# One turn per query block, and measured durations in the planner that orders the matmul engine's work

## The chip, the cores and the metric

The kernel runs on one core of a Trainium2 chip. The metric is the device time of one execution in microseconds (us), the median over repeated runs. The engines are named as in the profile: PE (TensorE, matmuls), PEld (its weight loads), DVE (VectorE), ACT (ScalarE), POOL (GpSimd), SP (SyncE, DMA issue).

## The reference

One decoder layer over 1024 positions of width 1024, in float32: a gated DeltaNet mixer (4 heads of 128) and a sparse attention mixer (8 heads of 64 in 2 groups) run side by side on the same normed input, are merged under two gates, and a SwiGLU feed-forward block follows.

```python
h = rms_norm(x, mix_norm_gain)
proj = jnp.einsum('bsd,de->bse', h, w_in)
...
o_a = gated_delta_rule_chunked(q_a, k_a, v_a, beta, log_decay)
...
q_n = partial_rope(q_b.reshape(...), pos) * (NSA_HEAD_DIM ** -0.5)
o_b = native_sparse_attention(q_n, k_cmp, v_cmp, k_slc, v_slc, k_win, v_win, gates, ...)
merged = (jax.nn.sigmoid(merge_a) * jnp.einsum('bse,ed->bsd', o_a, w_branch_gdn)
          + jax.nn.sigmoid(merge_b) * jnp.einsum('bse,ed->bsd', o_b, w_branch_nsa))
x = x + jnp.einsum('bsd,de->bse', merged, w_out)
```

The attention has three branches per block of 128 queries and group: 63 compressed blocks, the selected blocks (with 16 of 16 blocks chosen, that is all keys up to the query) and a window of 512. The scale 64 ** -0.5 is 0.125.

## The kernel before

Products are made at float32 accuracy from a high and a low part: `split` (L83) rounds a value to fp32r on ACT and subtracts it on DVE, and `mmk` (L144) multiplies high by high, high by low and low by high. Three matmuls of one such step, L147 to L149, are called a triple here.

The stages follow one another: norm and first projections; convolution inputs; the DeltaNet chunks; the compressed keys; attention; merge, output projection and feed-forward. Three of them, from some 205 to 925 us, are woven. PE is the one engine whose order the kernel writes itself (`manual_schedule`); the other engines' instructions are placed by a scheduler that takes them in the order in which the program issues them. In a woven stage several Python generators issue work, and `weave` (L205) decides which goes next by `Model` (L180), a small clock of the engines: a generator yields the time at which its next PE work can start, and `weave` takes the one with the earliest start. `m.run(engine, ready, duration)` (L187) books a duration on an engine and returns when the result is there. A filler, the last argument, goes in wherever it can start before all others. The fillers are triples of the projections (`projections`, L703, tile `pn`) and of the merge gates (`gates_half`, L717, tile `pm`), and `mm3g` (L155) tells the model what a triple costs. The durations are numbers in the code, and no time is measured when the kernel is built.

- In the DeltaNet stage `prepare_chunks` (L501) turns and normalises keys and queries of a chunk of 128 positions, `solve_chunks` (L606) makes three rounds of turn (X), product masked on DVE (Pm) and update (Y), `scan_chunks` (L632) carries the state, `turn_chunks` (L687) turns the result. The sums behind Y's start are made on DVE by many small instructions (Ut, Yb). `EV` (L499) is the model's time for an eviction.
- In the compressed stage `compressed` (L789) runs, with the filler; what is left of the projections and of the first half of the gates is issued without cover at its end.
- In attention `all_keys` (L960), `all_queries` (L989), `scores` (L1024), `transposes` (L1117) and `products` (L1146) are woven. A unit is one query block, group and branch. Its scores go to PSUM slots (tag S, six), DVE takes the maximum, ACT the exponential, POOL scales by one over the sum, PE turns the probabilities (`ppt`), `split` makes two parts and PE multiplies both with the values (`po`). At most three turned tiles may be pending. Up to 11 tiles of the second half of the gates (`aside`, L913) are the filler; four more come after attention.
- A query block (128 queries, 4 heads of one group) is loaded as `qraw`, rotated on POOL, scaled there, split into `qs` (twice the same 64 columns side by side, high and low part apart), turned by PE in two groups of four transposes (`pqt`), and copied by ACT into `qt`.

Of the kernel before, what the change touches and what calls it, by code (L numbers as in the profile page):

```python
# [11 lines left out]
F32 = mybir.dt.float32  # L12
# [3 lines left out]
ALU = mybir.AluOpType  # L16
# [17 lines left out]
def tile_hybrid(ctx: ExitStack, tc: tile.TileContext, a: dict, out: bass.AP, dbg=None):  # L34
# [252 lines left out]
    def hN(n):  # L287
        return lambda k: tuple(t[:, k, :] for t in hT2[n])
# [414 lines left out]
    def projections():  # L703
        for c0, n in segs:
            wh, wl = piece()
            for i in range(NT):
                pt = psM("pn")
                yield from mm3g(pt[:, :n], hT(i), lambda k: (wh[:, k, :], wl[:, k, :]), KD, 110)
                st = sp.tile([P, 320], F32, tag="zz", name="nst", bufs=2)
                nc.scalar.copy(st[:, :n], pt[:, :n])  # L710
                o = (i % 2) * P
                nc.gpsimd.dma_start(nsa_d[i // 2][o:o + P, c0 - SEG0:c0 - SEG0 + n], st[:, :n])
        yield from gates_half(0, psM)
# [3 lines left out]
    def gates_half(n, ptile):  # L717
        for pc_ in range(8):
            wh, wl = piece()
            for j in range(2):  # L720
                pt = ptile("pm")
                yield from mm3g(pt, lambda k: (wh[:, k, j * P:(j + 1) * P], wl[:, k, j * P:(j + 1) * P]),
                                hN(n), KD, 216)
                th = stage[0]("thm")
                nc.scalar.activation(th, pt, AF.Tanh, scale=0.5)  # L725
                nc.gpsimd.dma_start(gt_d[2 * pc_ + j][n], th)
                yield 0, 600 if n else 0
# [214 lines left out]
    with ExitStack() as ph:  # L942
# [17 lines left out]
        def all_keys():  # L960
            for i in range(NT):
# [16 lines left out]
                for g in range(2):  # L978
                    yield max(t0, slots["S"][0])
                    t = m.run("pe", max(t0, slots["S"].pop(0)), 120)  # L980
# [4 lines left out]
                    t = m.run("act", t, 270)  # L985
# [3 lines left out]
        def all_queries():  # L989
            for i in range(NT):  # L990
                for g in range(2):
# [9 lines left out]
                    qs = at_("qs", [P, 4, 2, 2, 64], 1, F32R)  # L1001
                    nc.gpsimd.tensor_scalar(raw, raw, 0.125, 1.0, op0=ALU.mult, op1=ALU.mult)
                    qv = qv[:, :, None, :].broadcast_to([P, 4, 2, 64])
                    split(qs[:, :, 0], qs[:, :, 1], qv)
# [6 lines left out]
                    t = m.run("act", m.t["pe"] + 4000, 480)  # L1011
                    t0 = m.run("dve", t, 600)
                    for l in range(2):
                        yield max(t0, slots["S"][0])
                        t = m.run("pe", max(t0, slots["S"].pop(0)), 230)
                        pt = pT("pqt2")
                        for h in range(4):
                            nc.tensor.transpose(pt[:, h, :], qs[:, h, l].bitcast(F32), ident)
                        nc.scalar.copy(qt[:, :, l, :], pt)
                        t = m.run("act", t, 480)  # L1020
                        slots["S"].append(t)
                    qts[2 * i + g] = (qt, ga, t)

        def scores():  # L1024
            for u, (i, g, br, j0, nk) in enumerate(units):
# [10 lines left out]
                if br == 0:  # L1036
# [10 lines left out]
                    t = m.run("dve", t, 340)  # L1047
# [4 lines left out]
                    t = m.run("act", t, 800)  # L1052
                    slots["S"].append(t)
                else:
                    b = 0 if br == 1 else 1
                    cuts = (0, w) if nk <= 4 else (0, (nk + 1) // 2 * P, w)
                    for n in range(len(cuts) - 1):
# [7 lines left out]
                        for h in range(4):  # L1065
# [4 lines left out]
                            t = m.run("pe", t, 2 * (c1 - c0) * 0.42 + 60)  # L1070
# [9 lines left out]
                            t = m.run("dve", t, (c1 - c0) * 1.05 + 70)  # L1080
                            t = m.run("act", t, (c1 - c0) * 0.83 + 140)
# [24 lines left out]
                for n in range(len(cuts) - 1):  # L1106
                    for h in range(4):
                        v = Ps[n][h]
                        nc.gpsimd.tensor_scalar(v, v, cs[:, h, n:n + 1], 1.0, op0=ALU.mult, op1=ALU.mult)  # L1109
                        t = m.run("pool", t, (cuts[n + 1] - cuts[n]) * 1.05 + 30)  # L1110
# [6 lines left out]
        def transposes():  # L1117
            po = None
            for u, (i, g, br, j0, nk) in enumerate(units):
# [4 lines left out]
                for j in range(nk):  # L1124
# [4 lines left out]
                    t = m.run("pe", max(t_p, slots["S"].pop(0)), 230)  # L1129
# [8 lines left out]
                    t = m.run("act", t, 480)  # L1138
                    t = m.run("dve", t, 600)
# [6 lines left out]
        def products():  # L1146
            po = None
            n = 0
            while n < sum(u[4] for u in units):
# [12 lines left out]
                if fin is not None:  # L1162
# [8 lines left out]
                    t = m.run("act", t, 480)  # L1171
                    t = m.run("dve", t, 600)
# [515 lines left out]
```

## Time and profile before

| | |
|---|---|
| median of 3 runs | 1800.11 us (1800.06 to 1801.05) |
| profiled execution | 1798.52 us |
| its span, first to last instruction | 1796.8 us |
| PE busy | 1722.6 us, 96% of the span, 9348 matmuls |
| PEld, DVE, ACT, POOL busy | 1458.3, 1096.6, 768.2, 641.4 us |
| mean granted clock of TensorE | 0.990 of full speed (2.4 GHz) |

A row of the profile names line, engine, operation, output and inputs of a group of instructions. Matmuls are pipelined and their ends are modelled, so printed durations of neighbours overlap: how long a matmul holds PE is read from the start of the next one. In the timeline, brackets give the idle time of the engine just before the row and what ended it. The granted clock is a mean over a stretch.

### The profile page before, as it was taken

What the parts mean: (1) busy time and instruction counts of PE and PEld (TensorE: products, weight loads), DVE (VectorE), ACT (ScalarE), POOL (GpSimd) and SP (SyncE); (2) the same over time, 40 slices, a digit from 0 to 9 for tenths busy, and PEclk for the clock granted to TensorE, in tenths of its full rate; (3) what the DMA queues carried; (4) which work ended last, traced back from release to release, by engine and by line L of the source; (5) the groups of instructions that cost most, each with busy time, mean ns of one, the idle gap of its engine ahead of it and who ended that gap; (6) DMA issues with size and microseconds to landing.
All of it is one profiled execution on the core that took longest, in us unless ns stands there. A gap on an engine that the chain in (4) does not pass through costs nothing.

```text
span 1796.8 us, 26109 instructions
## 1 busy us (share of the span) xinstructions
PE 1722.6 (96%) x9348; PEld 1458.3 (81%) x9348; DVE 1096.6 (61%) x2061; ACT 768.2 (43%) x1814; POOL 641.4 (36%) x1028
## 2 busy tenths in 40 slices
PE   7999989999999899999999999899999999989998
PEld 7888878989888677777778888688888888878886
DVE  6466566664543688677744434665555555678685
ACT  5244433343321698777732212433333333344452
POOL 3400144344231886675530211644444344210000
PEclk9999999999999999999999999899999999999999
DMA  6322444443473312011057350033333333572342
GB/s 208 99 96 95 143 118 110 109 121 78 110 194 105 107 34 60 25 42 39 13 178 227 109 201 1 13 120 113 95 104 119 95 106 100 186 276 85 100 140 100
DMA packets 183009, 196.40 MB, mean 109 GB/s; under 512 B 23408, under 2 KB 139360, under 8 KB 182880
## 3 DMA queue, kind: packets, MB, share of 16 engines
q1 hardware_dynamic: 164112, 162.03, 29.7%
q0 software_dynamic: 18560, 32.62, 6.1%
q8 instruction: 73, 1.20, 0.3%
q14 instruction: 56, 0.46, 0.1%
q10 hardware_dynamic: 208, 0.09, 0.0%
HBM read 139.01 MB, written 55.69 MB: 108 GB/s over the span
## 4 chain that ended last, share of the span: by engine, by line
PE 75%; issue 6%; DVE 6%; POOL 5%; ACT 3%; DMA 3%; SPq 0%; POOLq 0%; DVEq 0%; ACTq 0%
PE M L149 14%; PE M L147 14%; PE M L148 14%; PE s L1074 3%; PE ppt L1132 3%; PE pq L148 2%; PE pq L147 2%; PE pq L149 2%; PE po L1159 2%; PE po L1160 2%; PE pm L147 1%; DVE Ut L596 1%; PE pm L149 1%; PE pm L148 1%; PE py L627 1%
## 5 line engine op out<-in xcount | busy, mean ns | idle before, releaser
L85 ACT ACTIVATE ahi<-fraw 128x512 fp32r<-128x512 f32 x88 | 55.6, 633 | 142.0 <-PE M L148 140.1
L1079 ACT ACTIVATE Ps<-s,mx 128x384 f32<-128x384 f32 (+3 forms) x192 | 106.0, 560 | 23.7 <-DVE mx L1078 22.6
L86 DVE TENSOR_TENSOR ptl<-ppt,pth 128x512 fp32r<-128x512 f32 (+1 forms) x148 | 99.0, 683 | 25.0 <-ACT pth L85 24.7
L1109 POOL TENSOR_SCALAR Ps<-Ps,cs 128x384 f32<-128x384 f32 (+3 forms) x192 | 107.9, 580 | 13.3 <-ACT pth L85 5.3
L1078 DVE TENSOR_REDUCE mx<-s 128x1 f32<-128x384 f32 (+3 forms) x192 | 94.9, 514 | 19.0 <-PE s L1077 13.5
L1074 PE MATMUL s<-KT,qt 128*128 128x384 f32 (+3 forms) x384 | 99.3, 359 | 3.0 <-DVE ptl L86 1.8
L147 PE MATMUL pn<-whi,h 128*128 128x264 f32 (+1 forms) x320 | 100.6, 314 | 0.0
L85 ACT ACTIVATE pth<-ppt 128x512 fp32r<-128x512 f32 (+1 forms) x148 | 87.1, 604 | 23.7 <-PE ppt L1132 23.2
L147 PE MATMUL pm<-h,whi 128*128 128x512 f32 x224 | 96.4, 430 | 0.2 <-ACT thm L725 0.2
L148 PE MATMUL pn<-wlo,h 128*128 128x264 f32 (+1 forms) x320 | 91.4, 286 | 0.0
L149 PE MATMUL pn<-whi,h 128*128 128x264 f32 (+1 forms) x320 | 91.3, 285 | 0.0
L149 PE MATMUL pm<-h,wlo 128*128 128x512 f32 x224 | 88.5, 395 | 0.0
L148 PE MATMUL pm<-h,whi 128*128 128x512 f32 x224 | 88.1, 393 | 0.0
L85 ACT ACTIVATE ahi<-fsum 128x512 fp32r<-128x512 f32 x66 | 41.7, 633 | 107.8 <-PE M L148 107.8
L86 DVE TENSOR_TENSOR wlo<-wraw,whi 128x1024 fp32r<-128x1024 f32 (+1 forms) x50 | 61.1, 1232 | 41.2 <-ACT whi L85 39.5
L86 DVE TENSOR_TENSOR alo<-fraw,ahi 128x512 fp32r<-128x512 f32 x88 | 71.3, 811 | 23.5 <-ACT ahi L85 23.4
L1611 POOL TENSOR_TENSOR rms_r<-rms_ms,small 128x1 f32<-128x1 f32 x8 | 5.1, 646 | 209.2 <-DVE rms_ms L1609 209.2
L147 PE MATMUL M<-act,ahi 128*128 128x512 f32 x194 | 77.0, 397 | 2.7 <-ACT ahi L85 2.7
L1132 PE MATMUL ppt<-ident,Ps 128*128 128x128 f32 x528 | 77.7, 274 | 1.5 <-POOL Ps L1109 1.3
L148 PE MATMUL M<-act,ahi 128*128 128x512 f32 x194 | 76.9, 396 | 2.2 <-DVE act L86 2.2
L85 ACT ACTIVATE ahi<-ar 128x512 fp32r<-128x512 f32 x66 | 41.5, 630 | 83.7 <-PE M L148 44.9
L149 PE MATMUL M<-act,alo 128*128 128x512 f32 x194 | 77.0, 397 | 0.0
(509 smaller groups left out, 5515.2 us busy)
## 6 DMA issues: line engine op xcount, KB each, us to landing
wraw<-in_w_in_dram SPq DMA_DIRECT2D x50, 512.0 KB, 4.3
fraw<-in_w_gate_up_dram SPq DMA_DIRECT2D x44, 512.0 KB, 4.1
ar<-act_d SPq DMA_DIRECT2D x35, 512.0 KB, 3.5
act_d<-asum SPq DMA_DIRECT2D x44, 256.0 KB, 2.4
act_d<-act SPq DMA_DIRECT2D x33, 256.0 KB, 2.0
gt_d<-thm POOLq DMA_DIRECT2D x32, 256.0 KB, 2.8
gg<-gt_d SPq DMA_DIRECT2D x32, 256.0 KB, 2.9
qkv_d<-ac POOLq DMA_DIRECT2D x24, 256.0 KB, 2.3
```

The costliest lines, as they stand in the source:

```text
L85: nc.scalar.activation(hi, src, AF.Copy)
L86: nc.vector.tensor_tensor(lo, src, hi.bitcast(F32), op=ALU.subtract)
L147: nc.tensor.matmul(ps, ah, bh, start=first, stop=False)
L148: nc.tensor.matmul(ps, ah, bl, start=False, stop=False)
L149: nc.tensor.matmul(ps, al, bh, start=False, stop=last)
L1074: nc.tensor.matmul(s, qt[:, h, l, :], KT[g][:, b, j0 * P + c0:j0 * P + c1], start=l == 0, stop=l == 1 and not ext)
L1078: nc.vector.tensor_reduce(mx[:, h, n:n + 1], s, axis=AX.X, op=ALU.max, negate=True)
L1079: nc.scalar.activation(pr, s, AF.Exp, bias=mx[:, h, n:n + 1], accum_out=sums[:, h, n:n + 1])
L1109: nc.gpsimd.tensor_scalar(v, v, cs[:, h, n:n + 1], 1.0, op0=ALU.mult, op1=ALU.mult)
L1132: nc.tensor.transpose(pt[:k, h, :], prs[h][:, jj * P:jj * P + k], ident)
L1159: nc.tensor.matmul(po, v, th_, start=first, stop=False)
L1160: nc.tensor.matmul(po, v, tl_, start=False, stop=fin is not None)
```

## The change

Two things. A query block is no longer scaled on POOL and split before it is turned: one ACT copy scales it and writes it twice side by side, PE turns it once in full float32, and `split` makes the two parts as it leaves PSUM. And the numbers of the model change: the cost of a filler triple, and most durations of the attention stage.

```diff
-                yield from mm3g(pt[:, :n], hT(i), lambda k: (wh[:, k, :], wl[:, k, :]), KD, 110)
+                yield from mm3g(pt[:, :n], hT(i), lambda k: (wh[:, k, :], wl[:, k, :]), KD, 121)
...
-                                hN(n), KD, 216)
+                                hN(n), KD, 227)
...
-                    qs = at_("qs", [P, 4, 2, 2, 64], 1, F32R)
-                    nc.gpsimd.tensor_scalar(raw, raw, 0.125, 1.0, op0=ALU.mult, op1=ALU.mult)
-                    qv = qv[:, :, None, :].broadcast_to([P, 4, 2, 64])
-                    split(qs[:, :, 0], qs[:, :, 1], qv)
+                    qs = at_("qs", [P, 4, 2, 64], 1)
+                    nc.scalar.activation(qs, qv[:, :, None, :].broadcast_to([P, 4, 2, 64]), AF.Copy, scale=0.125)
...
-                    t = m.run("act", m.t["pe"] + 4000, 480)
-                    t0 = m.run("dve", t, 600)
-                    for l in range(2):
-                        yield max(t0, slots["S"][0])
-                        t = m.run("pe", max(t0, slots["S"].pop(0)), 230)
-                        pt = pT("pqt2")
-                        for h in range(4):
-                            nc.tensor.transpose(pt[:, h, :], qs[:, h, l].bitcast(F32), ident)
-                        nc.scalar.copy(qt[:, :, l, :], pt)
-                        t = m.run("act", t, 480)
-                        slots["S"].append(t)
+                    t0 = m.run("act", m.t["pe"] + 4000, 600)
+                    yield max(t0, slots["S"][0])
+                    t = m.run("pe", max(t0, slots["S"].pop(0)), 430)
+                    pt = pT("pqt2")
+                    for h in range(4):
+                        nc.tensor.transpose(pt[:, h, :], qs[:, h], ident)
+                    split(qt[:, :, 0, :], qt[:, :, 1, :], pt)
+                    t = m.run("act", t, 610)
+                    t = m.run("dve", t, 685)
+                    slots["S"].append(t)
...
-                            t = m.run("pe", t, 2 * (c1 - c0) * 0.42 + 60)
+                            t = m.run("pe", t, 2 * max(110, (c1 - c0) * 0.43 + 7) + 40 * len(ext))
...
-                            t = m.run("dve", t, (c1 - c0) * 1.05 + 70)
-                            t = m.run("act", t, (c1 - c0) * 0.83 + 140)
+                            t = m.run("dve", t, (c1 - c0) * 1.04 + 150)
+                            t = m.run("act", t, (c1 - c0) * 0.82 + 480)
...
-                        t = m.run("pool", t, (cuts[n + 1] - cuts[n]) * 1.05 + 30)
+                        t = m.run("pool", t, (cuts[n + 1] - cuts[n]) * 0.85 + 280)
...
-                    t = m.run("pe", max(t_p, slots["S"].pop(0)), 230)
+                    t = m.run("pe", max(t_p, slots["S"].pop(0)), 435)
...
-                    t = m.run("act", t, 480)
-                    t = m.run("dve", t, 600)
+                    t = m.run("act", t, 610)
+                    t = m.run("dve", t, 685)
```

The last pair stands in `transposes` and again in `products`; in `all_keys` 120 and 270 become 220 and 380, and in the compressed branch of `scores` 340 and 800 become 420 and 2000.

The numbers move the instructions. Three places are shown, each before and after the change; lines of the changed kernel from L1000 on are three lower.

First piece: DVE in the middle of the DeltaNet stage, where a chunk's keys and queries are normalised (ss, kh, qh) while an earlier chunk is solved (Pm, Y). Before:

```order
L86 TENSOR_TENSOR wlo<-wraw,whi 128x1024
L596 TENSOR_TENSOR Ut<-U,Yb_881 32x13x13
L86 TENSOR_TENSOR wlo<-wraw,whi 128x1024
L598 TENSOR_REDUCE Yb_881<-Ut 32x13
L539 SCALAR_TENSOR_TENSOR ss<-ss,rscale 128x8
L623 TENSOR_TENSOR Pm<-pp,LM 128x512
L596 TENSOR_TENSOR Ut<-U,Yb_881 32x14x14
L86 TENSOR_TENSOR at_4223<-pat,at_4222 128x512
L598 TENSOR_REDUCE Yb_881<-Ut 32x14
L544 TENSOR_TENSOR kh<-pk,rr 128x512
L596 TENSOR_TENSOR Ut<-U,Yb_881 32x225
L628 TENSOR_TENSOR Y<-Y,py 128x512
```

After:

```order
L596 TENSOR_TENSOR Ut<-U,Yb_881 32x14x14
L598 TENSOR_REDUCE Yb_881<-Ut 32x14
L623 TENSOR_TENSOR Pm<-pp,LM 128x512
L596 TENSOR_TENSOR Ut<-U,Yb_881 32x225
L539 SCALAR_TENSOR_TENSOR ss<-ss,rscale 128x8
L598 TENSOR_REDUCE Yb_881<-Ut 32x15
L544 TENSOR_TENSOR kh<-pk,rr 128x512
L86 TENSOR_TENSOR at_4148<-pat,at_4147 128x512
L546 TENSOR_TENSOR qh<-pqt,rr 128x512
L628 TENSOR_TENSOR Y<-Y,py 128x512
```

The two weight splits (wlo) have left the place ahead of Pm, ss has gone behind Pm, and qh stands ahead of Y.

Second piece: PE where attention starts, the first query block. Before, 16 triples of the gates stand ahead of it with no other work between, the last matmul of which is the first row:

```order
L149 MATMUL pm<-h_115,wlo 128x512
L1018 MATMUL pqt_5962<-ident,qs 128x128 x4
L1018 MATMUL pqt_5968<-ident,qs 128x128 x4
L147 MATMUL pm<-h_115,whi 128x512
L148 MATMUL pm<-h_116,whi 128x512
```

After, with 33 triples ahead:

```order
L149 MATMUL pm<-h_115,wlo 128x512
L1014 MATMUL pqt_5957<-ident,qs 128x128 x4
L147 MATMUL pm<-h_115,whi 128x512
L148 MATMUL pm<-h_116,whi 128x512
L149 MATMUL pm<-h_115,wlo 128x512
```

One group of four transposes is gone, and seventeen triples have come ahead of it.

Third piece: PE near the end of attention, where the turns of the last unit begin (`ppt` x12) after the last products of the unit before. Before:

```order
L1159 MATMUL po_10774<-pth,VS_5355 128x512
L1160 MATMUL po_10774<-ptl,VS_5355 128x512
L147 MATMUL pm<-h_115,whi 128x512
L148 MATMUL pm<-h_116,whi 128x512
L149 MATMUL pm<-h_115,wlo 128x512
L147 MATMUL pm<-h_115,whi 128x512
L148 MATMUL pm<-h_116,whi 128x512
L149 MATMUL pm<-h_115,wlo 128x512
L1132 MATMUL ppt<-ident,Ps 128x128 x12
L147 MATMUL pm<-h_115,whi 128x512
L148 MATMUL pm<-h_116,whi 128x512
L149 MATMUL pm<-h_115,wlo 128x512
```

After:

```order
L1156 MATMUL po_10707<-pth,VS_5289 128x512
L1157 MATMUL po_10707<-ptl,VS_5289 128x512
L1129 MATMUL ppt<-ident,Ps 128x128 x12
L1156 MATMUL po_10707<-pth,VS_5282 128x512
L1157 MATMUL po_10707<-ptl,VS_5282 128x512
L1129 MATMUL ppt<-ident,Ps 128x128 x4
L1156 MATMUL po_10707<-pth,VS_5283 128x512
L1157 MATMUL po_10707<-ptl,VS_5283 128x512
```

The triples are gone from here. Up to this stage's end the changed order has placed 82 triples in attention, before 81; the last of the changed order stands ahead of turn 106 of 148, and 25 of those of before stand behind that place.

## Rows read from the trace of the kernel before

**Rows 1.** Stretches: busy time (instructions) of PE, PEld, DVE, ACT, POOL; clock, DMA, GB/s.

```profile
205.00:516.00 311.00, 288.76 (x2187) 274.05 (x2186) 176.64 (x445) 112.39 (x336) 114.93 (x134) 0.98 0.43 115
592.00:846.40 254.40, 242.98 (x1576) 195.37 (x1577) 191.63 (x432) 205.96 (x659) 178.26 (x481) 0.99 0.18 47
846.40:925.00 78.60, 77.14 (x459) 61.39 (x458) 55.16 (x101) 53.35 (x145) 37.05 (x81) 1.00 0.15 45
```

**Rows 2.** Waits of PE, 205 to 516 us: us in total, times, longest.

```profile
PE py L627 <- DVE Pm L623: 10.9, 8, 2.3
...
PE px L616 <- DVE Y L628: 3.3, 3, 1.4
PE pp L621 <- ACT X L617: 2.3, 3, 1.0
```

**Rows 3.** Timeline of PE: start, duration, instructions; idle before, its end.

```profile
368.54 2.06 PE L627 MATMUL py<-Y,Pm 128*128 128x128 f32 x8 [2.25 <-DVE Pm L623]
...
400.58 1.16 PE L627 MATMUL py<-Y,Pm 128*128 128x128 f32 x8 [2.03 <-DVE Pm L623]
...
592.99 1.74 PE L1018 MATMUL pqt<-ident,qs 128*128 128x128 f32 x8 [3.70 <-ACT qs L85]
```

**Rows 4.** Stretches around these three waits, columns as in rows 1.

```profile
368.00:376.00 8.00, 7.46 (x51) 7.46 (x52) 2.96 (x5) 1.70 (x4) 6.45 (x7) 0.79 0.65 153
400.00:408.00 8.00, 7.42 (x63) 7.23 (x63) 4.95 (x10) 2.19 (x5) 7.20 (x8) 1.00 1.00 258
592.00:600.00 8.00, 6.94 (x31) 5.69 (x32) 1.92 (x6) 4.10 (x12) 4.95 (x20) 0.79 0.56 150
```

**Rows 5.** Groups by line and shape: busy us, mean ns of one; idle before.

```profile
L86 DVE TENSOR_TENSOR ptl<-ppt,pth 128x512 fp32r<-128x512 f32 x132 | 88.3, 683 | 23.5 <-ACT pth L85 23.2
...
L1018 PE MATMUL pqt<-ident,qs 128*128 128x128 f32 x128 | 19.4, 280 | 4.2 <-ACT qs L85 3.7 <-ACT Pc L1049 0.4
L1019 ACT CAST qt<-pqt 128x512 fp32r<-128x512 f32 x32 | 18.8, 610 | 1.3 <-PE pqt L1018 1.1
...
L86 DVE TENSOR_TENSOR qs<-qraw,qs 128x512 fp32r<-128x512 f32 x16 | 12.0, 748 | 11.0 <-ACT qs L85 10.5 <-PE ppt L1132 0.5
```

**Rows 6.** Timeline of PE: two groups of query transposes and what follows each.

```profile
602.76 0.66 PE L1018 MATMUL pqt<-ident,qs 128*128 128x128 f32 x4 [0.38 <-ACT Pc L1049]
603.18 0.42 PE L1074 MATMUL s<-KT,qt 128*128 128x128 f32 x2
...
603.50 0.61 PE L1018 MATMUL pqt<-ident,qs 128*128 128x128 f32 x4
603.87 0.42 PE L1074 MATMUL s<-KT,qt 128*128 128x128 f32 x2
```

**Rows 7.** Timeline of PE: two neighbouring matmuls of the merge gates.

```profile
901.21 0.39 PE L148 MATMUL pm<-h,whi 128*128 128x512 f32 x1
901.44 0.40 PE L149 MATMUL pm<-h,wlo 128*128 128x512 f32 x1
```

**Rows 8.** Timeline of PE: two neighbouring matmuls of the projections.

```profile
208.17 0.28 PE L149 MATMUL pn<-whi,h 128*128 128x264 f32 x1
208.29 0.28 PE L147 MATMUL pn<-whi,h 128*128 128x264 f32 x1
```

**Rows 9.** Timeline of PE: the two waits of the chunk at 430 us.

```profile
431.18 1.16 PE L627 MATMUL py<-Y,Pm 128*128 128x128 f32 x8 [2.05 <-DVE Pm L623]
...
435.52 0.66 PE L616 MATMUL px<-ident,Y 128*128 128x128 f32 x4 [1.39 <-DVE Y L628]
```

**Rows 10.** Timeline of PE and POOL: the end of attention.

```profile
899.95 0.23 PE L1077 MATMUL s<-maskD,identb 128*128 128x128 bf16 x1
...
904.34 5.37 POOL L1109 TENSOR_SCALAR Ps<-Ps,cs 128x512 f32<-128x512 f32 x8
...
910.21 1.47 PE L1132 MATMUL ppt<-ident,Ps 128*128 128x128 f32 x12
...
915.25 0.50 PE L1160 MATMUL po<-ptl,VS 128*128 128x512 f32 x1 [1.24 <-DVE ptl L86]
```

More of the change, by code (lines that the diff above doesn't have):

```diff
@@ L979, in all_keys @@
                     yield max(t0, slots["S"][0])
-                    t = m.run("pe", max(t0, slots["S"].pop(0)), 120)
+                    t = m.run("pe", max(t0, slots["S"].pop(0)), 220)
                     pt = pT("pkt")
@@ L984, in all_keys @@
                     nc.scalar.copy(KT[g][:, :, i * P:(i + 1) * P], pt[:, 0:2, :])
-                    t = m.run("act", t, 270)
+                    t = m.run("act", t, 380)
                     slots["S"].append(t)
@@ L1046, in scores @@
                     pr = at_("Pc", [P, 4, 64], 2)
-                    t = m.run("dve", t, 340)
+                    t = m.run("dve", t, 420)
                     for h in range(4):
@@ L1051, in scores @@
                     Ps.append([pr[:, h, :] for h in range(4)])
-                    t = m.run("act", t, 800)
+                    t = m.run("act", t, 2000)
                     slots["S"].append(t)
@@ L1170, in products @@
                                         .rearrange("t p c -> p t c"), o2[a0:a0 + 64])
-                    t = m.run("act", t, 480)
-                    t = m.run("dve", t, 600)
+                    t = m.run("act", t, 610)
+                    t = m.run("dve", t, 685)
                     slots["O"].append(t)
```

## The prediction

> **What bounds the kernel now.** I read the busy time of the engines stretch by stretch first. In each of the three stretches that the change touches, TensorE (PE) is the engine with the least left over [rows 1]: 288.76 of 311.00 us while the DeltaNet chunks run, 242.98 of 254.40 us in the first three quarters of attention, 77.14 of 78.60 us in its last part. ScalarE (ACT) comes nearest, 205.96 of 254.40. So a microsecond of PE work or of PE waiting is a microsecond of the kernel, and the other engines count only where PE waits for them.
>
> Second, the waits of PE. In the DeltaNet stretch it waits mostly for the three steps of a solve: 8 times for Pm, 3 times for Y, 3 times for X, 14 waits in all [rows 2]. In attention the longest single wait is the first one, 3.70 us for the query's high half, which ends at 592.99 [rows 3]. The stretch around it has a granted clock of 0.79 [rows 4]; so does the one at 368 us, where PE had waited 2.25 us [rows 3], while a wait of 2.03 us at 400 us left its stretch at 1.00 [rows 3, 4]. The two levels are 1.2 and 2.4 GHz, so a mean of 0.79 over 8 us costs (1 - 0.79) x 8 = 1.7 us of full-speed work each time.
>
> The profiled execution took 1798.52 us (span 1796.8, 1.7 us around it); the median of the runs is 1800.11, that is 1.6 higher. The sum is made on 1798.52 and moved up by 1.6.
>
> **Part 1, the queries.** For each of 16 query blocks PE turned two halves, four transposes each; now it turns one, so 64 of 128 transposes go. Their printed duration is 280 ns [rows 5], but they overlap: a group of four starts at 602.76 and the next matmul at 603.18, another at 603.50 and 603.87 [rows 6]. That is 0.42 and 0.37 us per group; I take 0.40, so 16 x 0.40 = **-6.3 us** (-5.9 to -6.7). The Trainium skill ("TensorE: Matmul & The Clock Gate", PE-mode transpose) gives about 275 ns for one transpose in a kernel's context; by that figure the 64 would be worth 17.6 us and the time 1783.8. The row's duration agrees with the page, and the row starts speak against adding the durations up.
>
> ACT loses one of three 128x512 passes per block: 16 x 0.61 us [rows 5]. The vector engine (DVE) now subtracts out of PSUM; the subtraction of the probabilities, which does that today, takes 683 ns against 748 ns for the present one [rows 5]. GpSimd (POOL) loses 16 scalings. All three I cost at nothing: they lie under PE's work, which fills 95% of that stretch. If that cover were gone, ACT's 9.8 us would be the gain there, more than the 6.3 and not instead of the waits below. The one PSUM slot is now held until the subtraction is done, but one slot is taken in place of two; nothing.
>
> **Part 2, the first query.** A filler step is one triple of matmuls of the merge gates or of the projections. Ahead of the first query's transposes now stand 33 triples with no other work between, where 16 stood (second order piece). A gate matmul takes 0.23 us from start to start [rows 7], a triple 0.69, so 11.7 us more work lies under the query's chain, which was 3.70 us late. The wait goes, and with it the slow stretch: -3.7 - 1.7 = **-5.4 us** (at least -3.7). The triples are not new work: as many are missing earlier, so they cost nothing themselves. What that takes from the earlier stretch is part 3.
>
> **Part 3, the DeltaNet chunks.** The model now takes a projection matmul for 121 units instead of 110, so where it put five triples between a step and the next it puts four; by the last preparation matmul 292 projection triples are done, where 312 were. Matmuls start 0.12 us apart [rows 8], so a triple is 0.36 us. Where PE had slack, nothing is lost. Where it waited, the wait grows by a triple: 14 waits [rows 2] x 0.36 = **+5.1 us**. The low end is 0. The high end is that nothing in the stretch gets shorter: 20 x 0.36 = 7.3, and two more falls of the clock like the one at 368, 3.4 together: +10.7. I take the middle, because the order of the vector engine also changes against it: in five of eight chunks Y now stands behind ss, kh, at and qh (first piece). The chunk at 430 us has that order today: there PE waits 2.05 us for Pm and then 1.39 for Y, with five triples under it [rows 9].
>
> **Part 4, attention.** It has as many triples as before (82 for 81) but spends them sooner: the last 25 of before lie behind the place where the changed order has used its last (third piece). In the first part PE sits idle 254.40 - 242.98 = 11.4 us [rows 1], 3.7 of it part 2's; of the other 7.7 I expect half to be covered by 25 more triples, **-4** (0 to -7.7). In the last part 25 x 0.69 = 17.3 us of fill go. PE's own work is then 77.14 - 17.3 = 59.8 us against 53.35 of ACT [rows 1]: PE still has the most to do, so most of the fill was not needed. What was: after the last score matmul, at 899.95, the last unit's turns can start when POOL has scaled four of its eight tiles; the eight take 5.37 us from 904.34, so four are done at 907.0, 7.1 us later [rows 10]. PE began them at 910.21 with seven triples (4.8 us) in between, so its own work there is 10.3 - 4.8 = 5.5: a wait of 1.6. Two more of about 1.2 as now stands at 915.25 [rows 10], behind the first turns and at the end, make 4.0, and I add 3 for scattered waits, since ACT is close. Of these 7.0 the present 1.46 is there already: **+5.5** (0 to 15.8, all 17.3 bare).
>
> Sum: -6.3 - 5.4 + 5.1 - 4 + 5.5 = **-5.1**, 1793.4 for the profiled execution, **1795.0** for the median. Differences below 0.2% (3.6 us) I call the same.
>
> **Rivals.**
> - *The DeltaNet stretch takes all back.* Part 3 at its high end, +10.7 in place of 5.1: 1800.6. For it: the five chunks in the order of the chunk at 430, where one more triple less makes two waits longer, and the clock fell once at 2.25 us. Against: 24 steps of each kind and only 14 waits.
> - *The fill is missing at the end (slower).* Every triple that went from the last part leaves PE bare, 15.8 in place of 5.5: 1805.3. The place is from 846 us on; it decides once the waits there pass 15.8 us in all (7.0 in my sum, 1.46 now), which is where the total comes out 3.7 above now. For it: turn, split, product is a chain through three engines and ACT has 53 us to do in what would be 60. Against: three tiles may be pending, so a product rarely stands right behind its own split.
> - *Both waits are cheap.* Part 3 at 0 and 2 in place of 5.5: 1786.4. For it: most steps have slack.
> - *The transposes are worth their printed time.* 64 x 0.280 = 17.9 in place of 6.3, 1783.4. For it, the duration in the row; against it, the row starts. (The page cited above has the same duration.)
> - *The change does not shorten any wait of attention by its new durations:* -4 becomes 0, 1799.0; with part 3 somewhat dearer this is the first rival's time, and I count it there.
>
> **How the numbers follow.** My forecast 0.45 (its own range 1789 to 1801), the DeltaNet rival with the last one 0.19, the missing fill 0.18, both cheap 0.12, printed time 0.06. Faster: 0.34 of the forecast, 0.12 and 0.06, 0.52. Same: 0.11 and 0.14 of the DeltaNet rival, 0.25. Slower: 0.18 and 0.05, 0.23. The range goes from 1785.5 to 1806: below it lie the printed time and a part of the cheap case, above it the missing fill with a falling clock on top, together under 0.2.
>
> **What would show it.** 64 transposes of the queries, no wait ahead of the first, clock 1.00 there; 16 scaled copies of some 0.6 us on ACT and 16 subtractions near 0.68 us; in the DeltaNet stretch waits for Pm and Y of over 1 us in five chunks; in attention few waits up to four fifths and some 7 us after. If the waits after the last filler pass 16 us, or the clock falls in several chunks, the forecast is wrong on the slow side; if the DeltaNet stretch waits no longer than now, on the fast side.

## The result, and the profile after

The changed kernel took 1825.71 us (1822.58 to 1832.51 in four runs) beside 1800.58 us for the kernel before on the same chip: a ratio of 1.0156, 95% interval 1.0136 to 1.0175. It is 25 us slower. The prediction was 1795.0, with 1785.5 to 1806 as its range. The profiled execution took 1826.83 us, span 1825.1, mean granted clock 0.979 (before 0.990).

The program's stages can be cut at rows of TensorE's (PE) timeline: the first `pvt`, the last `pat`, the last `pcmp`, the first query transpose, the last `po` of attention. In brackets stand the triples of the merge gates in each.

| us | before | after |
|---|---|---|
| DeltaNet | 301.1 (60) | 301.4 (44) |
| compressed keys | 61.5 (60) | 63.8 (58) |
| to the first query | 15.3 (16) | 27.0 (33) |
| attention | 330.4 (81) | 347.3 (82) |

Seventeen of the triples ahead of the first query are moved work (17 x 0.69 = 11.7 us of the 11.7). So the loss is the 16 triples that DeltaNet no longer holds in the same time, 2.3 us and two triples in the compressed stage, and 17 us in attention, in spite of the 6 us of transposes that went. What stands ahead of and behind these four stages became 2.9 us shorter.

Busy time and clock by stretch, in the columns of [rows 1]:

```profile
205.00:516.00 311.00, 281.96 (x2139) 269.13 (x2138) 173.72 (x443) 109.53 (x332) 118.28 (x132) 0.97 0.42 111
516.00:579.00 63.00, 60.30 (x264) 50.59 (x263) 27.82 (x70) 14.94 (x24) 13.09 (x37) 0.95 0.57 161
...
606.50:846.40 239.90, 222.67 (x1341) 178.65 (x1342) 166.75 (x375) 172.97 (x558) 146.37 (x407) 0.93 0.20 53
846.40:954.00 107.60, 102.36 (x627) 81.15 (x626) 80.88 (x157) 80.58 (x229) 61.55 (x140) 0.98 0.09 25
```

Attention up to 846 had a clock of 0.99 [rows 1] and has 0.93: 0.07 x 239.9 = 16.8 us of full-speed work at most, since a low clock costs nothing while PE waits. PE is idle 17.2 us there.

**DeltaNet.** The waits of PE, 205 to 516 us, as in [rows 2]:

```profile
PE px L616 <- DVE Y L628: 13.6, 9, 2.2
PE py L627 <- DVE Pm L623: 7.4, 6, 1.5
```

The waits for Y went from 3.3 to 13.6, those for Pm from 10.9 to 7.4. DVE's timeline in the chunk at 400 us shows why:

```profile
395.95 0.67 DVE L623 TENSOR_TENSOR Pm<-pp,LM 128x512 f32<-128x512 f32 x1
...
398.94 0.69 DVE L544 TENSOR_TENSOR kh<-pk,rr 128x512 f32<-128x512 f32 x1 [1.46 <-POOL rr L541]
399.54 0.68 DVE L86 TENSOR_TENSOR at<-pat,at 128x512 fp32r<-128x512 f32 x1
400.14 0.68 DVE L546 TENSOR_TENSOR qh<-pqt,rr 128x512 f32<-128x512 f32 x1
400.74 0.68 DVE L628 TENSOR_TENSOR Y<-Y,py 128x512 f32<-128x512 f32 x1
```

Y stands behind kh, which waits 1.46 us for GpSimd's (POOL) power, and behind two passes more. PE waits 2.21 us for it. Behind this wait, and behind its like at 368 and 436 us, the clock is at the low level for part of a stretch (columns as above):

```profile
368.00:376.00 8.00, 7.52 (x54) 7.52 (x54) 1.12 (x2) 2.56 (x5) 3.57 (x5) 0.79 0.54 121
400.00:408.00 8.00, 6.53 (x43) 6.53 (x44) 2.11 (x4) 2.09 (x4) 3.50 (x5) 0.79 0.54 115
432.00:440.00 8.00, 5.78 (x36) 5.58 (x37) 3.13 (x7) 0.96 (x2) 5.81 (x6) 0.79 0.57 119
```

Before, only the first of the three had fallen [rows 4]; from 432 to 440 us the clock was 1.00 then. From 205 to 516 us PE's idle time went from 22.2 [rows 1] to 29.0 us.

**The first query.** Its wait is still there, behind 33 triples in place of 16. PE's wait, then two rows of SyncE's DMA queue (SPq), then POOL:

```profile
606.55 0.65 PE L1014 MATMUL pqt<-ident,qs 128*128 128x128 f32 x4 [3.89 <-ACT qs L1002]
...
597.93 0.34 SPq L966 DMA_DIRECT2D kraw<-nsa_d  x1
598.32 0.43 SPq L997 DMA_DIRECT2D qraw<-nsa_d  x1
...
597.78 1.04 POOL L118 TENSOR_SCALAR whi<-wraw 128x1024 fp32r<-128x1024 f32 x1 [3.75 <-PE pm L148]
...
599.51 1.49 POOL L118 TENSOR_SCALAR whi<-wraw 128x1024 fp32r<-128x1024 f32 x1
...
605.59 0.25 POOL L787 TENSOR_TENSOR qraw<-rope 128x32 f32<-128x32 f32 x1
```

The same loads in the kernel before:

```profile
583.88 0.34 SPq L966 DMA_DIRECT2D kraw<-nsa_d  x1
584.27 0.43 SPq L997 DMA_DIRECT2D qraw<-nsa_d  x1
```

The query's load is issued 14 us later and its transposes start 13.6 us later. What sets the load's time is the load of the keys (`kraw`), which stands just ahead of it in SP's queue. SP's queue waits 6.2 us with it, for a gate matmul of PE (us in total, times, longest):

```profile
SPq L966 <- PE pm L149: 6.2, 1, 6.2
```

That matmul, and its like in the kernel before:

```profile
597.51 0.39 PE L149 MATMUL pm<-h,wlo 128*128 128x512 f32 x1
...
583.46 0.39 PE L149 MATMUL pm<-h,wlo 128*128 128x512 f32 x1
```

The keys' load follows the end of it by 0.03 us in both. It is the last matmul of the 128th gate triple, with which the first half of the gates ends. The code gives a reason: attention's tiles come from a pool that is opened behind `ph1.close()`, and this frees the half of the input (`h`) that these triples read. So the moved triples do not lie under the query's chain: they stand ahead of its start. Under it lie the last 7 triples (4.8 us; before, 8 and 5.5), and from the start of the chain to the transposes it is 8.6 us (9.1 before), so about the same wait is left. On POOL two roundings of weights (whi) stand ahead of the rotation too, and the buffers they wait for are freed by PE's own gate matmuls (`3.75 <-PE pm`). More cover delayed what it was to cover.

**Attention.** The longest wait, PE's and then what DVE and POOL did ahead of it:

```profile
629.43 1.09 PE L1129 MATMUL ppt<-ident,Ps 128*128 128x128 f32 x4 [4.87 <-POOL rope L89]
...
625.89 2.79 DVE L119 TENSOR_TENSOR wlo<-wraw,whi 128x1024 fp32r<-128x1024 f32 x1 [5.03 <-POOL whi L118]
628.60 0.68 DVE L86 TENSOR_TENSOR qt<-pqt,qt 128x512 fp32r<-128x512 f32 x1
629.20 0.47 DVE L1075 TENSOR_REDUCE mx<-s 128x1 f32<-128x128 f32 x2
...
623.45 1.40 POOL L1106 TENSOR_SCALAR Ps<-Ps,cs 128x128 f32<-128x128 f32 x4
624.83 1.03 POOL L118 TENSOR_SCALAR whi<-wraw 128x1024 fp32r<-128x1024 f32 x1
```

The profile names POOL's rope as what ended it, but POOL had been busy without a gap. DVE stood 5.03 us at the low part of weights (`wlo`) that a later gate needs, until POOL came to the high part. Behind it queued the subtraction of the third query block (`qt`), one of the 16 that the change brings to DVE's work on PSUM, then the maxima (`mx`) of scores that were done, and ACT's exponentials behind those. In the trace PE's sequencer stands at a semaphore of DVE's, which moved at 629.29, as that subtraction ended. In the code turns and query blocks share the six PSUM slots (tag S), and a query block's slot is now held until the subtraction is done. Behind this wait PE runs at the low level (0.50, 1.2 GHz; columns as in [rows 1]):

```profile
628.00:634.50 6.50, 5.07 (x16) 4.24 (x17) 5.73 (x15) 3.60 (x17) 4.76 (x14) 0.50 0.61 163
```

The other low stretches up to 846 us stand behind waits of 3.89 (the first query), 2.59 at 647.83 (a gate triple waits for ACT to empty the one gate tile), 2.24 and 3.07 us; behind one of 1.75 at 752.33 the clock stayed at 1.00. At 802 us a like queue stands on ScalarE (ACT):

```profile
802.10 1.11 PE L1129 MATMUL ppt<-ident,Ps 128*128 128x128 f32 x4 [3.07 <-ACT Ps L1076]
...
799.94 0.31 ACT L85 ACTIVATE kt<-kraw 128x128 fp32r<-128x128 f32 x1 [4.53 <-POOL kraw L787]
...
801.39 0.56 ACT L1076 ACTIVATE Ps<-s,mx 128x384 f32<-128x384 f32 x1
```

ACT stands at the split of the next key block until POOL has rotated it, with the exponentials of the present scores behind. The waits of 2.24 us at 685.96 and of 1.75 at 752.33 are of this kind too.

After the last triple, from 886.5 us on, PE waits little:

```profile
PE po L1156 <- DVE osum L1165: 2.0, 2, 1.3
PE ppt L1129 <- POOL Ps L1106: 0.9, 3, 0.3
PE po L1157 <- DVE ptl L86: 0.8, 3, 0.4
```

### The profile page after: what moved, and what is told of

Same layout as the page of the kernel before. It is cut to its first block, busy times and chain, and to the rows that moved or that the text cites. A ratio compares the mean times of both kernels' runs of the same rounds, so it can differ in the third digit from the quotient of the medians.

```text
span 1825.1 us, 25962 instructions
## 1 busy us (share of the span) xinstructions
PE 1733.5 (95%) x9284; PEld 1467.0 (80%) x9284; DVE 1099.6 (60%) x2061; ACT 764.1 (42%) x1798; POOL 639.1 (35%) x1012
## 4 chain that ended last, share of the span: by engine, by line
PE 75%; issue 6%; DVE 6%; POOL 5%; ACT 3%; DMA 3%; SPq 0%; POOLq 0%; DVEq 0%; ACTq 0%
PE M L149 14%; PE M L147 14%; PE M L148 14%; PE ppt L1129 3%; PE s L1071 3%; PE pq L148 2%; PE pq L147 2%; PE pq L149 2%; PE pm L147 2%; PE po L1156 2%; PE pm L148 2%; PE pm L149 2%; PE po L1157 2%; DMA E<-gc_d 1%; DVE Ut L596 1%
## 5 line engine op out<-in xcount | busy, mean ns | idle before, releaser
L147 PE MATMUL pm<-h,whi 128*128 128x512 f32 x224 | 99.2, 443 | 3.3 <-ACT thm L725 3.3
L148 PE MATMUL pm<-h,whi 128*128 128x512 f32 x224 | 90.9, 406 | 0.0
L1129 PEld LDWEIGHTS ppt<-ident,Ps 128*128 128x128 f32 x528 | 64.9, 145 | 24.9 <-issue 7.3
```

Source lines behind the costliest of these rows:

```text
L147: nc.tensor.matmul(ps, ah, bh, start=first, stop=False)
L148: nc.tensor.matmul(ps, ah, bl, start=False, stop=False)
L1129: nc.tensor.transpose(pt[:k, h, :], prs[h][:, jj * P:jj * P + k], ident)
```

## The experiments

Each ratio is to the kernel before, run on the same chip, with its 95% interval. "Net attention" is attention's length less 0.69 us for each gate triple in it: 274.5 before (330.4 - 81 x 0.69), 290.7 after. It is read from one execution of each kernel. Executions of one kernel differ by up to 12 us (run 4, 1797.9 to 1810.2), so a few us in that column say nothing alone. Where fewer than 81 or 82 triples are left for attention (69 in runs 4, 9 and 17, 78 in run 15), the others run without cover after it.

**1 to 4: which part costs.** The query code alone (the diff without its number lines outside `all_queries`); the filler's cost alone; the changed kernel with the one set of numbers or the other put back.

```diff
# 1: from the changed kernel, every number of the model outside all_queries as before
# 2: from the kernel before
-... KD, 110)          +... KD, 121)
-... hN(n), KD, 216)   +... hN(n), KD, 227)
# 3: the changed kernel with 2 undone;  4: with the attention stage's durations undone
```

> The kernel before with the new query code and its own planner steps alone; every other planner number as before. Theory A (the loss comes from the two sets of numbers, and one turn per query block is a gain): 64 transposes less, about -6.3, so 1794, with waits of attention as before. Rival B (the query code itself makes the waits of attention, since its slot of PSUM is held through ScalarE and then VectorE): attention longer by some 13 us of waits and 5 of low clock less 6, so 1812. Rival C (the cost of the filler alone does everything): 1794, as A.

> The kernel before with the filler's cost alone changed (121 and 227 for 110 and 216), old query code and old attention numbers. Theory A: 16 gate triples fewer in a DeltaNet stage of the same length, +10.5, and +1.8 in the compressed stage, so 1813, and attention as before. Rival B: the same 1813. Rival C: the whole loss and the 6 that the queries give back, so 1832, with waits of over 2 us in the first 80 us of attention.

> The changed kernel with the filler's cost put back to 110 and 216; new query code and new attention numbers stay. Theory A: the DeltaNet and compressed stages return to before (-12), attention keeps its loss, so 1813. Rival B: 1813 as well. Rival C: everything but the queries returns, 1794.

> The changed kernel with the durations of the attention stage put back, the filler at 121 and 227 and the new query code. Theory A: DeltaNet's and the compressed stage's loss stay (+12), the queries give 6, so 1806, with no wait over 2 us inside attention but the first. Rival B: attention's waits stay, 1824. Rival C: they stay too, 1826.

| | ratio | us | DeltaNet (triples) | net attention |
|---|---|---|---|---|
| 1 query alone | 0.9976 (0.9958 to 0.9993) | 1795.7 | 300.3 (60) | 272.3 |
| 2 filler alone | 1.0110 (1.0093 to 1.0128) | 1819.6 | 301.9 (44) | 283.3 |
| 3 filler old | 1.0056 (1.0037 to 1.0075) | 1809.9 | 301.2 (60) | 284.3 |
| 4 attention old | 1.0028 (1.0015 to 1.0042) | 1804.0 | 303.2 (44) | 264.9 |

The filler's cost makes DeltaNet lose its 16 triples in both kernels that have it, and in none that has not. Theory A holds for the stages ahead of attention, and rival B falls for the query code alone, which makes the kernel faster; in the changed kernel the longest wait of attention did end at its subtraction. In attention no theory holds: the filler's cost moved net attention by +8.8 with the old query code, by -7.4 with the new, and by +6.4 with all the new durations. Runs 2 and 4 differ by the query code alone, and by 15.7 us, of which 6.3 is PE's work; the rest came along with another order.

The query code gained 4 us where 6.3 were expected; the interval, 1.3 to 7.6 us, holds 6.3 as well. One wait came with it. Run 1, DVE and PE:

```profile
611.60 2.69 DVE L119 TENSOR_TENSOR wlo<-wraw,whi 128x1024 fp32r<-128x1024 f32 x1 [4.98 <-POOL whi L118]
...
615.04 0.69 PE L1071 MATMUL s<-KT,qt 128*128 128x128 f32 x2 [4.12 <-ACT Ps L1076]
```

**5: the first query's load ahead of the drained gates.** The first blocks' loads, rotation and copies are issued ahead of the gates that run without cover.

```diff
-    drain(rest)
...
+        early = []
+        for st in (all_keys(), all_queries()):
+            early.append(chain([next(st)], st))
+        drain(rest)
...
-        weave(m, [all_keys(), all_queries(), products(), ...
+        weave(m, early + [products(), ...
```

The tiles that this needs come from a pool of their own, so they need no memory that the gates' first half frees.

> The changed kernel, with the first block's keys and queries loaded, rotated and scaled before the gates that are issued without cover ahead of attention (their loads then stand in SyncE's queue ahead of those gates' weights); the matmul order is the same up to there. Theory D (the wait for the first query stayed because its load and rotation stand in the queues behind the weight loads and roundings of the very triples that were to cover it): the wait of 3.9 falls below 0.3 and the clock there is 1.00, worth 3.9 and some 3 of low clock, 1819. Rival E (the chain from load to scaled copy is itself what is late, for what it reads): the wait stays over 2 us, 1825.

Ratio 1.0128 (1.0090 to 1.0166), 1818.35 us. The wait is gone and the clock stays up; the last triple and the query's transposes (line 1008 in run 5), and the stretches around:

```profile
599.64 0.39 PE L149 MATMUL pm<-h,wlo 128*128 128x512 f32 x1
599.87 0.60 PE L1008 MATMUL pqt<-ident,qs 128*128 128x128 f32 x4
...
592.00:600.00 8.00, 8.00 (x38) 6.58 (x37) 2.45 (x2) 0.61 (x1) 3.11 (x3) 1.00 0.34 107
600.00:608.00 8.00, 7.01 (x51) 5.92 (x49) 2.58 (x7) 3.97 (x10) 2.03 (x7) 1.00 0.54 170
```

In the changed kernel the 8 us from 608 on had a granted clock of 0.62. The stage ahead of the query takes 22.95 us in place of 27.0, attention 4.0 less. The query's load is issued at 540.14 us, 58 us ahead of its place in the changed kernel. The intervals of the two ratios overlap; the stage and the row show that the wait came from the late load. Of theory D the time holds (1819 expected), and that the chain stood behind the very triples that were to cover it. The run changes the loads' place and their memory at once; that they had waited for a gate matmul, and not for weight loads in the queue, is read from the wait of SP's queue above, and the memory is the code's reason for it.

**6: EV with the filler's cost.**

```diff
-    EV = 1750
+    EV = 1925
```

> The changed kernel with EV, the planner's time for an eviction in the DeltaNet stage, raised with the filler's cost from 1750 to 1925, so that five triples fit again where the changed kernel places four (14 places with five, against 15 before and 2 in the changed kernel). Theory F (the stage lost its time because the real triple and the real eviction stayed the same while one triple less lay under each step): the stage takes 301 us with 59 gate triples in it in place of 44, its waits 22 us in place of 28.5, so about -10.5 and 1815. Rival G (the loss comes from the order of VectorE, which puts the normalising of keys and queries ahead of Y): the waits for Y of 2.2 us stay and the stage becomes longer with its 15 more triples, 311 us, no gain, 1825.

Ratio 1.0092 (1.0062 to 1.0121), 1815.75 us. DeltaNet takes 299.9 us with 59 triples. Its waits and the three stretches:

```profile
PE py L627 <- DVE Pm L623: 6.8, 5, 1.8
PE px L616 <- DVE Y L628: 4.0, 6, 1.4
...
368.00:376.00 8.00, 7.29 (x63) 7.06 (x62) 3.17 (x5) 2.62 (x5) 6.47 (x8) 1.00 0.64 165
400.00:408.00 8.00, 7.41 (x61) 7.10 (x60) 3.58 (x6) 3.09 (x6) 7.06 (x8) 1.00 0.85 220
432.00:440.00 8.00, 6.77 (x56) 6.67 (x57) 2.37 (x5) 2.62 (x5) 6.03 (x7) 1.00 0.44 90
```

Theory F's time holds, with all three clocks back. Rival G is not wholly apart from it: with five triples under a step again, the scheduler also orders DVE otherwise (at 400 us Y runs at 400.79 ahead of kh and qh). The fill and the order that follows from it were not tried one without the other.

**7, 8, 12 to 14: which durations of attention cost.** All on run 1 (the query code alone): 7 adds the numbers of turns and products, 8 those of scores, compressed branch and POOL, 12 the compressed branch's alone (420, 2000), 13 and 14 the same with 1400 and 2600.

```diff
# 12; 13 and 14 with 1400 and 2600
-                    t = m.run("dve", t, 340)
+                    t = m.run("dve", t, 420)
-                    t = m.run("act", t, 800)
+                    t = m.run("act", t, 2000)
```

> The kernel with the query code alone (1795.7), and of the planner's new durations only those of the turns and products (435, 610, 685). Theory H (the durations of scores, exponentials and POOL's scalings carry attention's loss of 14, because each of a unit's four scalings now adds 0.85 of its width and 280 on top of a step of 400 between engines: 3.2 us for four of 128 columns that take 1.4): no loss here, 1797. Rival I (the turns' durations carry it): 1809. Rival J (no number carries it, any change of the order moves attention by some 10 us either way): something that fits neither, and the two parts do not add up to 14.

> The kernel with the query code alone (1795.7), and of the new durations only those of the scores, the compressed branch and POOL's scalings. Theory H: all of the loss, 1809. Rival I: none, 1796. Rival J: neither, and together with the run of the turns' durations not 14.

> The kernel with the query code alone (1795.7), and of the score side's new durations only those of the compressed branch (340 to 420, 800 to 2000). The score side as a whole gave 1804.7. If the 2000, which stands for four exponentials that take some 1.2 us, carries it: 1803. If the scores' and GpSimd's durations carry it: 1796.

> The query code alone with the compressed branch's numbers at 420 and 1400, between 800 (1795.7) and 2000 (1802.3). If the loss is a property of the number (theory P: the planner holds one of six slots longer than the chip does and all streams queue behind it), it lies between, 1798 to 1800. If it is scatter of the order (rival Q), it is as likely outside: below 1796 or above 1802.

> The same with 2600. Theory P: more than at 2000, 1805 or above. Rival Q: anything from 1794 to 1806, without order.

| | ratio | us | net attention |
|---|---|---|---|
| 7 turns | 0.9981 (0.9962 to 1.0001) | 1795.15 | 271.5 |
| 8 scores | 1.0027 (1.0010 to 1.0044) | 1804.7 | 281.6 |
| 12 compressed, 2000 | 1.0019 (1.0008 to 1.0030) | 1802.3 | 278.8 |
| 13 compressed, 1400 | 0.9959 (0.9940 to 0.9977) | 1793.05 | 270.2 |
| 14 compressed, 2600 | 1.0003 (0.9984 to 1.0022) | 1799.1 | 277.0 |

Run 7 moved nothing and run 8 took 9 of the 14 us that theory H gave it; the two numbers of `all_keys` are in neither run. After 8 and 12 it looked as if the compressed branch's 2000 carried it. With 800, 1400, 2000, 2600 the net attention is 272.3, 270.2, 278.8, 277.0: it does not rise with the number, as theory P wanted. Rival Q (scatter of the order) is the better reading: the four span 9 us.

**11 and 16 to 18: the pass at which DVE stands.** Run 11 moves the low part of the second half's weights to POOL (on run 1); runs 16 to 18 move the high part to DVE instead, which leaves PE's order as it is: 16 in the changed kernel, 17 in run 9, 18 in run 10 (both below).

```diff
# 11
-                nc.vector.tensor_tensor(lo[...], raw, hi[...].bitcast(F32), op=ALU.subtract)
+                nc.gpsimd.tensor_tensor(lo[...], raw, hi[...].bitcast(F32), op=ALU.subtract)
# 16, 17, 18
-                nc.gpsimd.tensor_scalar(hi[...], raw, 1.0, 1.0, op0=ALU.mult, op1=ALU.mult)
+                nc.vector.tensor_copy(hi[...], raw)
```

> The kernel with the query code alone (1795.7), with the low parts of the second half of the gates' weights subtracted on GpSimd, where the high parts are rounded, instead of on VectorE. Theory M (the wait of 4.1 at 615 is VectorE standing at such a subtraction for 5.0 until GpSimd comes to the rounding, with a score's maximum queued behind): the wait goes and the low clock after it, 1790. Rival N (GpSimd, with 16 more passes of a 128x1024 tile, becomes late for the scalings of the probabilities): the wait is replaced by waits for scaled probabilities, 1796 or more.

Run 11: ratio 0.9994 (0.9976 to 1.0012), 1798.9 us; rival N holds. The 4.12 went, a wait of 3.80 for POOL's scaling came, and the first query waits longer, because a subtraction of 2.3 us now stands inside its rotation. POOL, and PE:

```profile
590.70 2.33 POOL L119 TENSOR_TENSOR wlo<-wraw,whi 128x1024 fp32r<-128x1024 f32 x1
...
595.97 1.11 PE L1014 MATMUL pqt<-ident,qs 128*128 128x128 f32 x4 [7.08 <-ACT qs L1002]
```

> The changed kernel, TensorE's order untouched, with the high parts of the second half of the gates' weights rounded on VectorE instead of GpSimd, so that VectorE no longer stands at a low part until GpSimd comes to the high part. Theory R (what attention loses follows how long VectorE stands there: 8.6 us in the kernel before, 13.6 in the changed one, 1.5 in the fastest so far): VectorE's idle time ahead of these passes falls below 4, the waits of 4.9 and 3.1 go and the clock with them, 1814. Rival S (VectorE, with some 16 passes of 1 us more, is late for the splits of the turned probabilities instead; or the waits belong to the order of TensorE): no gain or a loss, 1824 or more.

Run 16: ratio 1.0099 (1.0071 to 1.0126), 1818.0 us. In attention DVE idles 2.6 us ahead of these passes, for buffers that PE frees (13.6 in the changed kernel, 8.6 before), the waits of 4.87 and of 1.75 us are gone, and attention takes 341.1 us in place of 347.3. What is left there, the first query's wait with it:

```profile
PE pm L147 <- ACT thm L725: 3.3, 2, 2.6
PE ppt L1129 <- ACT Ps L1076: 3.2, 1, 3.2
PE pqt L1014 <- ACT qs L1002: 3.1, 1, 3.1
```

So theory R is right for 6 of the 17 us (by the ratios the gain is 10, and some 6 either way). It had put down the wait at 802 to the same cause; that one stayed (3.19), and the trace shows the key block's split on ACT there. Moving the key loads was not tried.

**9, 10, 15 and again 17, 18: the causes taken out together.** 9: the changed kernel with attention's durations as before, EV 1925, early load. 10: run 7 with the early load. 15: run 9 with the turns' numbers new.

> The changed kernel with the three causes found so far taken out together: attention's durations as before, EV at 1925, and the first block's keys and queries loaded ahead of the gates without cover. If the causes stand apart (theory K) their shares add up: 1804.0 with attention's old durations, less 10 for EV, less 7 for the first query, so 1787, below the kernel before by 0.6%. If they are one and the same loss told three ways, or a new order of attention takes it back (rival L), it is 1795 or more.

> The query code, the turns' and products' new durations, everything else of the planner as before, and the early load of the first block. Theory K: 1795.2 less 7, so 1788, no wait at the first query. Rival L: 1795, because attention waits at the first weight split instead.

> The fastest so far (1788.6: attention's old durations, EV at 1925, the first block loaded early) with the turns' and products' new durations added, which by themselves moved nothing (1795.2 against 1795.7). Theory P: no change, 1788, 0.6% below the kernel before. Rival Q: moved by 5 or more either way.

> The fastest so far (1788.6) with the same edit. Its VectorE stands there for only 1.5 us, so by theory R no gain: 1788. Rival S: 1792 or more, from VectorE's added passes.

> The kernel with the query code, the turns' durations and the early load (1789.8) with the same edit; its wait of 4.1 at 613 stands at such a pass. Theory R: that wait goes and the low clock with it, 1784. Rival S: 1790 or more.

| | ratio | us | net attention |
|---|---|---|---|
| 9 | 0.9944 (0.9924 to 0.9963) | 1788.6 | 265.7 |
| 10 | 0.9954 (0.9940 to 0.9968) | 1789.75 | 270.9 |
| 15 | 0.9977 (0.9963 to 0.9990) | 1794.6 | 273.5 |
| 17 | 0.9921 (0.9902 to 0.9940) | 1784.4 | 263.7 |
| 18 | 0.9939 (0.9920 to 0.9958) | 1787.05 | 268.0 |

Run 9 shows that EV and the early load add up (theory K), 1788.6 where 1787 was expected: no wait at the first query, 59 triples in 301 us of DeltaNet. Run 10 has the early load without EV, which its old filler's cost does not need: 1789.75 for 1788, with 60 triples in 305 us; run 1's wait of 4.12 is still there, at 613.06. In run 18 that one is gone, but PE waits 2.65 us at 761.45 instead, and the time lies between theory R's 1784 and rival S's 1790. Run 15 lost 6 us with numbers that had moved nothing in run 7, again rival Q. Run 17 is the fastest: 0.8% below the kernel before, with the filler's measured costs and the new query code, and without the other new durations. It gained 4 on run 9 where none was expected, but the intervals overlap.

## Why the prediction was wrong

The profiled execution took 1826.8 us where the sum has 1793.4. The step that failed by most is part 4's "half to be covered by 25 more triples", and behind the first query the sum has no term for attention's clock. The runs showed more waits and a low clock instead, 21 of the 33 us. Part 2 brings 5.4, part 3 5.6 and the compressed stage 3.7; the stages around are 2.9 better.

- **Part 1, the queries (-6.3): right in its rows, smaller in time.** (16 x 0.40 is 6.4.) 64 transposes, 16 copies and 16 subtractions are there, the subtraction 684 ns (683 was taken from the split of the probabilities). Alone they gave a ratio of 0.9976, 4 us. Not all that was put at nothing cost nothing: run 1 has a new wait of 4.12 us behind DVE, and the step "one slot is taken in place of two; nothing" failed in the changed kernel, where the wait of 4.87 us ended at the subtraction that holds the slot. The rival that the transposes are worth their printed time (17.9) falls with it.

```profile
L1014 PE MATMUL pqt<-ident,qs x64: 270/273/476, 606.6 to 894.1; 128*128 128x128 f32 x64
...
L86 DVE TENSOR_TENSOR qt<-pqt,qt 128x512 fp32r<-128x512 f32 x16 | 10.9, 684 | 3.8 <-ACT qt L85 3.7
```

- **Part 2, the first query (-5.4): wrong, nothing came of it.** The step "11.7 us more work lies under the query's chain" took the chain's start as fixed. It is not: the chain starts with the end of the gates' first half, so the moved triples stand ahead of it, and the wait is 3.89 us for 3.70. Run 5 frees the load from that, and the same 33 triples cover the chain. I had not followed the query's load back to what releases it.
- **Part 3, DeltaNet (+5.1): the mechanism right, the size at its high end.** Sixteen gate triples (11.0 us) less two projection triples (0.7) in a stage 0.35 us longer is +10.7, the bound that was worked out as 20 triples and two more falls of the clock. The middle was taken "because the order of the vector engine also changes against it"; PE's idle time grew by 6.8 us where 5.1 was the sum and 7.3 the bound, and the two more falls of the clock, 3.4, which only the bound had, came too. Run 6 took it back, the fill and DVE's order together. This is the first rival's term; its total missed for what follows.
- **The compressed stage (not in the sum): +2.3 us and two triples, 3.7 in all.** Its wait for a load is 2.69 in place of 1.92 us, and its clock 0.95 in place of 1.00. It has the same wait in every run (1.4 to 3.6 us); no run tried it.
- **Part 4, early (-4): wrong in sign.** More triples early did not cover the waits: up to 846 us PE idles 17.2 us behind the first query where 7.7 stood before and 4 fewer were forecast, and the low clock, at nothing in this part, costs up to 16.8. Every 16 triples bring a weight piece with four passes on POOL and DVE, and every eight an eviction on ACT, none of which I had costed; the longest wait stands at such a pass. Attention's net length grew by 16.2 where -6.3 - 4 + 5.5 = -4.8 was forecast: that is 21 of the miss. Run 16 accounts for 6. The new durations bring 12.0 of net attention with the filler's old cost (run 3 less run 1) and 25.8 with its new one (the changed kernel less run 4); which of them do it stays open, and the waits named above are read from the trace alone. The runs 12 to 15 show 6 to 9 us of scatter between orders.
- **Part 4, late (+5.5): too dear.** After the last triple PE waits 3.7 us. The rival "the fill is missing at the end" had the sign of the result, but not its place: it decides at 15.8 us from 846 on, where PE now waits about 5.
- **The range.** Its upper end added falls of the clock to one rival; no rival had the fill itself make waits, nor parts 2 and 4 failing together with part 3 at its high end.

## What to carry to other kernels

A planner's numbers act by their ratios: a filler's cost corrected without the step time that it is fitted into (EV) costs fill where the chip had not changed. Filler is not only matmuls: its weight loads, roundings and evictions stand in order in the queues of engines that the planner does not book, so before counting it as cover, follow the covered chain back to what releases its first load: here it was a matmul of the cover itself, through memory that is used again. And where a planner orders by hand, time two or three values of any number before believing one: orders that hold the same work differed here by 6 to 9 us.

## What the hardware showed that was not expected

A short POOL pass takes as long as the DVE pass beside it. A step of a rotation, 128x32, takes 0.25 us elsewhere; here it begins 0.06 us after a subtraction on DVE and ends just behind it. DVE, then POOL, in the changed kernel:

```profile
798.03 1.21 DVE L119 TENSOR_TENSOR wlo<-wraw,whi 128x1024 fp32r<-128x1024 f32 x1
...
798.09 1.25 POOL L92 TENSOR_TENSOR qraw<-rope 128x32 f32<-128x32 f32 x1
```

The other way round, the subtraction took 2.69 us at 611.60 in run 1, with a rounding on POOL inside it, and 1.21 at 614.42. And the rounding moved cheaply: 1.05 us on POOL, 0.69 on DVE (run 16), while the subtraction took 2.4 on POOL (run 11) against 1.2 on DVE.
